# Weight and mixed-row loads on ScalarE's queue, norm factors in the tile of the matrices to invert, a second buffer for masked operands, and the order by measured durations

## Chip, core and metric

The kernel runs on one core of a Trainium2 chip. The metric is the device time of one execution in microseconds (us), median of several runs. TensorE is called PE, its weight loads PEld, VectorE DVE, ScalarE ACT, GpSimd POOL and SyncE SP. PEq, ACTq or SPq before an operation means that the engine's sequencer issued it (a DMA, for example) and the engine's arithmetic stayed free. Each engine takes its instructions strictly in the order in which they stand in its own list.

## What is computed

One layer of a hybrid decoder for 1024 prompt tokens and 64 sample tokens (8 sequences of 8), all float32, with 1024 features:

```python
h = rmsnorm(x) * norm1_g
proj = h @ w_in                                   # 1024 -> 1536 (convolution) + 1792 (RWKV)
y_conv = c_b * conv3(c_c * c_x)                   # 512 columns
r, k, v, pw, pa, pg = split(lerp(p_rw, previous token, mu))
decay, a, g = small low-rank products of pw, pa, pg
for t in tokens:                                  # per head, 8 heads of 64
    S = S * decay_t - (S @ kk_t) x (kk_t * a_t) + v_t x k_t
    y_t = S @ r_t
y_rwkv = (groupnorm(y) + bonus) * g               # 512 columns
x = x + concat(y_conv, y_rwkv) @ w_out
h2 = rmsnorm(x) * norm2_g
x = x + relu(h2 @ w_ff1) ** 2 @ w_ff2             # 1024 -> 4096 -> 1024
out = rmsnorm(x) * normf_g
```

The outputs also hold the last convolution rows, the last projected row and the final states S.

## The kernel before

Each float32 product is made of three passes over rounded parts (`passes`): high times high, high times low, low times high. A weight is therefore loaded raw (`wraw`, 256 KB each), ACT writes its rounded copy `whi`, and DVE writes the rest `wlo` (`gen_load`, `gen_split`). The activations `h_hi` and `h_lo` stay in SBUF, 8 blocks of 128 features by 1088 tokens. Tokens are cut in three groups of 384, 384 and 320 (`GROUPS`). A piece of a projection is 24 matmuls into one of two PSUM banks (tag `mm`, tile `acc`), and a generator of the piece (`post_rkv`, `post_conv_c`, `post_out`, `relu2`) empties it.

The recurrence runs in chunks of 64 tokens. A unit `u` is a pair of heads `p` and a token group `g`; there are 12, in the order of `UN` (unit 0 is p 0, g 0; unit 11 is p 3, g 2), and units 2, 5, 8 and 11 also carry the 8 sample sequences. For a unit `gen_ew` makes the elementwise operands and the chunks' triangular matrices `LT`. Those go to DRAM (`lt_d`) and come back as `M`, one small matrix a partition (`SP.dma_start(M[24 * i:24 * i + nb], lt_d[:nb])`, L920). POOL inverts them in 31 pairs of instructions (`wtmp`, `W`, L1016 and L1018, `gen_invert`); SP stores the result (`w_d`, L1023) and brings it back as `Tt` (L1042, `gen_merge`). There is one tile `M`. `gen_recur` then walks through the chunks: PE writes `rc`, DVE takes `X` from it, PE goes on, ACT scales `UT` (L1100) and prepares `GD` (L1092), PE adds, and DVE writes the new state `Gh`. One chunk's result is the next one's operand. After the chunks PE writes `py`, and `gen_finish` normalizes it (its product `gt` goes to the DRAM matrix `mix_d`; `pty` is its transpose on PE). `gen_sample` handles the 8 sequences: for each half of them it masks two operands (`VM`, L1203) and multiplies each (`pgs`, L1210). The tile `VM` has one buffer, which the prompt's last state `So` and the operand `XY` also use.

After the last units, `gen_rows` loads the rows of `mix_d` that ACT and DVE split into `h_hi` and `h_lo` again (`mr`, L1299, 18 loads of 160 or 192 KB; `gen_mixed`, `split_row`). The output projection (PE, L659) adds to `x1`, whose old values `gen_norm2` loads (`x`, L1341). `gen_norm2` then frees the pools of the recurrence, opens new ones, and loads the norm factors `gB` (512 KB, L82), which `gen_xn` multiplies in (`xn`, L374). `gen_h` transposes `xn` on PE (`pt`, L394), and the MLP follows. From about 790 us on, the MLP's loops are written plainly and have no planner.

The order of all instructions up to there comes from a planner, `Weave`: every generator yields `ck(engine, cost)` before it issues an instruction, and the planner takes whichever step can start first by those costs, its credits of buffers (`acq`) and marks (`deps`). The costs are numbers written in the source. All DMAs named above stand on SP's queue. `wv.dma(kb)` charges SP 0.5 for one.

Of the kernel before, what the change touches and what calls it, by code (L numbers as in the profile page):

```python
# [9 lines left out]
F32 = mybir.dt.float32  # L10
# [6 lines left out]
D = 1024  # L17
# [16 lines left out]
def tile_kernel(ctx: ExitStack, tc: tile.TileContext, io: dict):  # L34
# [204 lines left out]
    def lerp(acc, m, g, out, acq=()):  # L239

        s, n = GROUPS[g]
        npr = n if g < 2 else 256
        mu = vec("mu", m)
        yield ck("ACT", 0.45, acq=acq, deps=["vec", "mss"] if g == 2 else ["vec"])
        out = out()
        A.activation(out[:, :n], acc[:, :n], AF.Copy, scale=omu[:, m:m + 1])
        yield ck("DVE", 0.65 + 0.075 * g)
# [288 lines left out]
    def split_row(k, g, src):  # L536

        s, n = GROUPS[g]
        yield ck("ACT", 0.42)
        A.copy(h_hi[:, k, s:s + n], src)  # L540
        yield ck("DVE", 0.5, nb=True)
        V.tensor_tensor(h_lo[:, k, s:s + n], src, h_hi[:, k, s:s + n].bitcast(F32), op=ALU.subtract)
        wv.mark(("hr", g, k))

    def post_conv_c(j, g):
        def f(acc):
            s, n = GROUPS[g]
            yield ck("ACT", 0.38)
            if g == 0:
                cs["cc"] = pa.tile([128, NT], F32, tag="cc", name="cc")  # L550
                cs["up"] = pa.tile([128, SEQ + 2], F32, tag="up", name="up")
                cs["us"] = pa.tile([128, NB, TB + 2], F32, tag="us", name="us")
                V.memset(cs["up"][:, 0:2], 0.0)
                V.tensor_copy(cs["us"][:, :, 0:2], scT[:, :, :, j])
            A.copy(cs["cc"][:, s:s + n], acc[:, :n])
        return f

    def post_conv_x(j, g):
        def f(acc):
# [4 lines left out]
            yield ck("DVE", 0.5)  # L564
# [9 lines left out]
            for x in (1, 2):  # L574
                yield ck("DVE", 0.5)
# [7 lines left out]
    def post_conv_b(j, g):  # L583
        def f(acc):
            s, n = GROUPS[g]
            cc = cs["cc"]
            yield ck("DVE", 0.5)
# [46 lines left out]
    def gen_split(loads):  # L634

        for ld in loads:
            for i, (pl, t, src) in enumerate(ld.parts):
                yield ck("ACT", 0.55, acq=("w" + t,), deps=[("raw", id(ld), i)] + START.pop(0))
                hi, lo = (pl["pq"].tile(list(src.shape), F32R, tag=n + t, name=n, bufs=WB[t]) for n in ("whi", "wlo"))
                A.copy(hi, ld.raw[i])  # L640
                yield ck("DVE", 0.6, nb=True)
# [3 lines left out]
                wv.free("wra" + t, after=1.0)  # L645
# [85 lines left out]
    def gen_open():  # L731

        yield ck("NO", 0, deps=[(nm, p, g) for nm in ("w2", "a2", "g2") for p in range(4) for g in range(3)] + ["masks"])
        plx.close()
        at["pp"] = pp = pool("pp", ppx)
# [6 lines left out]
        at["M"] = pp.tile([96, 32, 32], F32, name="M")  # L742
# [69 lines left out]
    def gen_ew(u):  # L812
# [7 lines left out]
        yield ck("DVE", 0.5, deps=[("sgta", u)])  # L820
# [18 lines left out]
        yield ck("DVE", 0.99, deps=[("xk", p, g)] + ([("pb", u - 2)] if u > 1 else []))  # L839
# [5 lines left out]
        yield ck("DVE", 0.5, deps=[("ptk", u - 1)] if u else [])  # L845
# [3 lines left out]
        yield ck("DVE", 0.5)  # L849
        q = Em  # L850
        V.scalar_tensor_tensor(q[:, :n], xk[:, :n], vec("kk", p), Em[:, :n], op0=ALU.mult, op1=ALU.mult)
        yield ck("DVE", 0.5)
# [5 lines left out]
        yield ck("DVE", 1.0, deps=done(u - 3) + ([("B", u - 2)] if u > 1 else []))  # L858
# [7 lines left out]
        yield ck("DVE", 0.6, deps=[("xr", p, g)])  # L866
# [37 lines left out]
        yield ck("SP", 0.9)  # L904
# [12 lines left out]
        yield ck("SP", 1.8, nb=True, deps=[("inv", u - 1)] if u else [])  # L917
# [5 lines left out]
        wv.now += 1.8  # L923
        wv.mark(("M", u))

    def gen_tokens(u):
# [31 lines left out]
        yield ck("DVE", 0.5, deps=[("A", u)])  # L958
# [4 lines left out]
        yield ck("ACT", 0.42)  # L963
        rk_hi = at["pe"].tile([128, 384], F32R, tag="kx", name="rk_hi")
        A.copy(rk_hi[:, :n], kp[:, :n])  # L965
        yield ck("DVE", 0.5)
# [8 lines left out]
        yield ck("DVE", 0.5)  # L975
# [18 lines left out]
    def gen_invert(u):  # L994
# [30 lines left out]
        wv.now += 1.8  # L1025
        wv.mark(("w_d", u))

    def gen_merge(u):
# [5 lines left out]
        yield ck("SP", 1.4, lat=5.5, deps=[("w_d", u)] + done(u - 2))  # L1034
# [103 lines left out]
    def gen_sample(u):  # L1138
# [59 lines left out]
        for b0 in range(0, NB, 4):  # L1198
            bs = slice(b0, b0 + 4)
            for x, tok in enumerate((VT, UT)):  # L1200
                yield ck("DVE", 0.35)
                VM = at["pp"].tile([128, 4, 64], F32, tag="VM", name="VM", bufs=1)
                V.tensor_tensor(VM, tok[:, c:c + 1, :].broadcast_to([128, 4, 64]),  # L1203
                                bmask[:, bs].unsqueeze(2).broadcast_to([128, 4, 64]), op=ALU.mult)
                if x == 0:
                    yield ck("PE", 0.43, acq=("rec",))
                    pg = ps.tile([128, 512], F32, tag="rec", name="pgs", bufs=2)
                else:
                    yield ck("PE", 0.43)
                PE.matmul(pg[:, 0:256], KT[:, c, x, :], VM.rearrange("p b v -> p (b v)"), start=(x == 0), stop=(x == 1))  # L1210
# [25 lines left out]
    def gen_finish(u):  # L1236
# [21 lines left out]
        yield ck("POOL", 1.3, lat=3.0)  # L1258
# [13 lines left out]
        yield ck("DVE", 0.5)  # L1272
# [3 lines left out]
        yield ck("DVE", 0.5)  # L1276
# [28 lines left out]
    def gen_rows():  # L1305

        for tag, k in ROWS:
            yield ck("SP", 0.5, acq=(tag,), deps=[("T", 10), ("mixd", 6), ("convd", 2, 0)])
# [8 lines left out]
        for g in (1, 2):  # L1317
            for _, k in ROWS:
                yield ck("SP", 0.5, acq=("mraw",), deps=[("mixd", 6 + g)])
                load_row(late["pq"].tile([128, 384], F32, tag="mr", name="mr", bufs=2), g, k)  # L1320

    def gen_mixed():

        for g in range(3):
            yield ck("NO", 0, lat=0, deps=[("acc", nmain - 3 + g)])
            for _, k in ROWS:
                yield ck("NO", 0, lat=0, deps=[("mr", g, k)])
                yield from split_row(k, g, raws.pop((g, k))[:, :GROUPS[g][1]])
                if g:
                    wv.free("mraw")  # L1330
# [155 lines left out]
    pb, p5 = late["pb"], late["p5"]  # L1486
# [110 lines left out]
    gF = pb.tile([128, D], F32, tag="gB", name="gF")  # L1597
# [61 lines left out]
```

## Time and profile before

| | us |
|---|---|
| three runs | 1537.56, 1539.78, 1541.71 |
| median | 1539.78 |
| profiled execution, its own time | 1538.91 |
| its span (first to last instruction) | 1537.0 |

| engine | busy us | share of the span |
|---|---|---|
| PE | 1461.7 | 95% |
| PEld | 1371.2 | 89% |
| DVE | 823.3 | 54% |
| ACT | 508.2 | 33% |
| POOL | 315.7 | 21% |

A share is a mean over stages with different limits. The span in 40 slices tells the stages apart: a digit is tenths of the slice, and the row PEclk is the TensorE clock that was granted, in tenths of full speed. In the trace a wait of a computing engine stands in brackets behind an instruction, with what ended it; a DMA instruction's time on SPq or ACTq is the time to issue it, not the transfer.

### The profile page before, as it was taken

The numbers are of one execution on the slowest core, as the hardware profiler recorded it, in microseconds if no ns is written. First come the engines' busy times: TensorE is split into PE (matmuls) and PEld (weight loads), VectorE is DVE, ScalarE is ACT, GpSimd is POOL, SyncE is SP. The second block draws the span as 40 slices with busy tenths as digits, with TensorE's granted clock in tenths as the row PEclk, the third lists the DMA queues.
The fourth block names the chain that finished last, engine by engine and source line by source line (L and its number), as shares of the span: only waits on it lengthen the run. The fifth ranks groups of instructions, "written<-read, shape, count | busy, mean of one in ns | idle before, by whom it ended". The sixth has DMA issues, their size and how long they took to land.

```text
span 1537.0 us, 25899 instructions
## 1 busy us (share of the span) xinstructions
PE 1461.7 (95%) x10163; PEld 1371.2 (89%) x10163; DVE 823.3 (54%) x1784; ACT 508.2 (33%) x1094; POOL 315.7 (21%) x855
## 2 busy tenths in 40 slices
PE   7999889989989999888999999999999999999997
PEld 5999779878878899788999999999999999999996
DVE  6538547856655777465644444434434344444447
ACT  6532233232323334243452223322223322233225
POOL 4023661564555446200000000000000000000004
PEclk9999859999977999898999999999999999999999
DMA  5343202321221233444321101111111111011103
GB/s 184 104 149 93 59 19 70 88 67 42 72 68 45 57 97 105 148 139 156 99 74 49 42 28 56 55 41 42 30 53 55 44 54 41 28 56 55 35 1 117
DMA packets 140292, 108.25 MB, mean 70 GB/s; under 512 B 43901, under 2 KB 131081, under 8 KB 140170
## 3 DMA queue, kind: packets, MB, share of 16 engines
q1 hardware_dynamic: 109546, 91.38, 19.9%
q10 hardware_dynamic: 30624, 15.21, 3.4%
q8 instruction: 80, 1.31, 0.4%
q14 instruction: 42, 0.34, 0.1%
HBM read 88.46 MB, written 18.09 MB: 69 GB/s over the span
## 4 chain that ended last, share of the span: by engine, by line
PE 76%; POOL 10%; DVE 4%; DMA 3%; issue 3%; SPq 2%; ACT 1%; POOLq 0%; DVEq 0%; ACTq 0%
PE acc L103 23%; PE acc L1524 16%; PE acc L652 13%; PE acc L1536 7%; PE acc L659 6%; POOL W L1018 5%; POOL wtmp L1016 5%; DMA M<-lt_d 1%; PE py L1120 1%; SPq L1023 1%; PE pw L507 1%; PE pm L885 1%; PE rc L1098 1%; PE rc L1102 1%; SPq L920 1%
## 5 line engine op out<-in xcount | busy, mean ns | idle before, releaser
L652 PE MATMUL acc<-h_hi,whi 128*128 128x384 f32 (+1 forms) x672 | 230.6, 343 | 7.1 <-DVE mp L253 6.2
L103 PE MATMUL acc<-h_lo,whi 128*128 128x320 f32 (+1 forms) x720 | 234.8, 326 | 0.0
L103 PE MATMUL acc<-h_hi,wlo 128*128 128x320 f32 (+1 forms) x720 | 234.8, 326 | 0.0
L103 PE MATMUL acc<-h_hi,whi 128*128 128x320 f32 (+1 forms) x720 | 234.7, 326 | 0.0
L652 PE MATMUL acc<-h_lo,whi 128*128 128x384 f32 (+1 forms) x672 | 229.9, 342 | 2.2 <-DVE h_lo L405 2.2
L652 PE MATMUL acc<-h_hi,wlo 128*128 128x384 f32 (+1 forms) x672 | 231.4, 344 | 0.0
L1526 DVE TENSOR_TENSOR x<-acc,x 128x512 f32<-128x512 f32 (+1 forms) x193 | 132.8, 688 | 124.9 <-PE acc L1524 124.9
L1402 DVE TENSOR_TENSOR slo<-r,shi 128x384 fp32r<-128x384 f32 (+1 forms) x96 | 51.5, 537 | 204.2 <-ACT shi L1400 204.2
L1570 POOL TENSOR_TENSOR rsf<-rsf,nhalf 128x1 f32<-128x1 f32 (+1 forms) x9 | 8.0, 888 | 741.3 <-DVE rsf L1567 740.2
L1016 POOL TENSOR_TENSOR wtmp<-W,M 96x60 f32<-96x60 f32 (+24 forms) x372 | 121.0, 325 | 168.0 <-DMA M<-lt_d 93.8
L1524 PE MATMUL acc<-f2h,shi 128*128 128x512 f32 (+1 forms) x386 | 150.2, 389 | 0.0
L1524 PE MATMUL acc<-f2h,slo 128*128 128x512 f32 (+1 forms) x386 | 150.0, 389 | 0.0
L1524 PE MATMUL acc<-f2l,shi 128*128 128x512 f32 (+1 forms) x386 | 149.9, 388 | 0.0
L652 PEld LDWEIGHTS acc<-h_hi,whi 128*128 128x128 f32 x672 | 130.1, 194 | 9.1 <-ACT rk_hi L965 7.6
L103 PEld LDWEIGHTS acc<-h_lo,whi 128*128 128x128 f32 x720 | 135.1, 188 | 0.6
L103 PEld LDWEIGHTS acc<-h_hi,whi 128*128 128x128 f32 x720 | 135.1, 188 | 0.6
L103 PEld LDWEIGHTS acc<-h_hi,wlo 128*128 128x128 f32 x720 | 135.2, 188 | 0.0
L68 ACT CAST f2h<-f2r 128x1024 fp32r<-128x1024 f32 x32 | 31.9, 1047 | 309.1 <-PE acc L1524 309.1
L652 PEld LDWEIGHTS acc<-h_lo,whi 128*128 128x128 f32 x672 | 129.8, 193 | 3.2 <-DVE h_lo L405 2.4
L652 PEld LDWEIGHTS acc<-h_hi,wlo 128*128 128x128 f32 x672 | 129.7, 193 | 1.5
L1018 POOL TENSOR_TENSOR W<-W,wtmp 96x60 f32<-96x60 f32 (+24 forms) x372 | 122.0, 328 | 29.1
L1396 ACT ACTIVATE r<-acc 128x384 f32<-128x384 f32 (+1 forms) x96 | 45.3, 472 | 150.3 <-PE acc L103 141.1
(303 smaller groups left out, 2895.6 us busy)
## 6 DMA issues: line engine op xcount, KB each, us to landing
f2r<-in_w_ff SPq DMA_DIRECT2D x32, 512.0 KB
wraw<-in_w_ff ACTq DMA_DIRECT2D x58, 256.0 KB
wraw<-in_w_in SPq DMA_DIRECT2D x52, 256.0 KB
wraw<-in_w_out SPq DMA_DIRECT2D x48, 256.0 KB
xt<-in_x_prompt SPq DMA_DIRECT2D x8, 512.0 KB
x<-in_x_prompt SPq DMA_DIRECT2D x8, 512.0 KB
out_y_prompt<-out SPq DMA_DIRECT2D x7, 512.0 KB
M<-lt_d SPq DMA_DIRECT2D x32, 96.0 KB
```

The source lines that it names most:

```text
L68: A.copy(hi, src)
L103: PE.matmul(acc[:, :n], a, b, start=(i == 0), stop=(i == 23))
L507: PE.matmul(pw[:, :n], a, b, start=(i == 0), stop=(i == m - 1))
L652: PE.matmul(acc[:, :n], a, b, start=(k == i == 0), stop=(k == 7 and i == 2))
L659: PE.matmul(acc[:n, :256], a, b, start=(k == i == 0), stop=(k == 7 and i == 2))
L1016: G.tensor_tensor(tv, W[:, 0:nr, r:r + 1].broadcast_to([96, nr, wd]), M[:, r:r + 1, r + 1:32].broadcast_to([96, nr, wd]), op=ALU.mult)
L1018: G.tensor_tensor(W[:, 0:nr, r + 1:32], W[:, 0:nr, r + 1:32], tv, op=ALU.subtract)
L1396: A.activation(r[:, :n], acc[:, :n], AF.Relu)
L1402: V.tensor_tensor(lo, r[:, :n], hi.bitcast(F32), op=ALU.subtract)
L1524: PE.matmul(acc[:, :cn], a, b, start=(j == 0), stop=(j == 3 * FB - 1))
L1526: V.tensor_tensor(x1[t][:, cols], acc[:, :cn], x1[t][:, cols], op=ALU.add)
L1536: PE.matmul(acc[:, :n], a, b, start=(j == 0), stop=(j == 3 * FB - 1))
```

## The change

`gen_load` puts the weight loads on ACT's queue, all but those of the first two projections (4 loads). The planner charges 0.05 for the issue and keeps its own clock for the transfers (`dma_a`). The 18 loads of mixed rows move to ACT in the same way. A permanent tile `gM` takes the place of `M` and of the two tiles for norm factors: the matrices to invert are its first 96 partitions, the factors of the second norm are loaded into it once the last inversion is done, and those of the final norm later. In `gen_sample` the second masked operand goes into half of `Sn` or `G0`, which hold nothing that is needed then, and both products are issued together. Around the inversion the planner no longer holds SP for 2.5 us: the mark `inv` stands at the inversion's end, and the store of `W` follows as a step of its own 2.5 us later. Some 45 costs in the planner's table are other numbers.

```diff
-        yield ck("ACT", 0.45, acq=acq, deps=["vec", "mss"] if g == 2 else ["vec"])
+        yield ck("ACT", 0.58 if g < 2 else 0.5, acq=acq, deps=["vec", "mss"] if g == 2 else ["vec"])
...
+        def dma_a(self, kb=192):
+
+            self.clk["DMA"] = max(self.clk["DMA"], self.now + 0.65) + kb / 360
+            return self.clk["DMA"] + 1.05
...
     def gen_load(loads):
 
+        for x, ld in enumerate(loads):
+            for i, (pl, t, src) in enumerate(ld.parts):
+                if x < 2:
+                    yield ck("NO", 0, acq=("wra" + t,))
+                else:
+                    yield ck("ACT", 0.05, lat=0, acq=("wra" + t,))
+                raw = pl["pq"].tile(list(src.shape), F32, tag="wraw" + t, name="wraw", bufs=2)
+                (SP if x < 2 else A).dma_start(raw, src)
...
-                wv.free("wra" + t, after=1.0)
+                wv.free("wra" + t, after=1.2)
...
+        at["gM"] = pool("pg", ctx).tile([128, D], F32, name="gM")
...
-        at["M"] = pp.tile([96, 32, 32], F32, name="M")
+        at["M"] = at["gM"][:96].rearrange("p (s t) -> p s t", t=32)
...
-        yield ck("DVE", 0.5, deps=[("sgta", u)])
+        yield ck("DVE", 0.95, deps=[("sgta", u)])
...
-        yield ck("SP", 2.5)
         wv.mark(("inv", u))
+        yield ck("NO", 0, lat=2.5)
+        yield ck("SP", 1.8)
         w_d = dp.tile([24, 32, 32], F32, tag="w_d", name="w_d", bufs=3)
...
+            VM = [at["pp"].tile([128, 4, 64], F32, tag="VM", name="VM", bufs=1), (G0 if b0 else Sn)[:, 0:4, :]]
             for x, tok in enumerate((VT, UT)):
-                yield ck("DVE", 0.35)
-                VM = at["pp"].tile([128, 4, 64], F32, tag="VM", name="VM", bufs=1)
-                V.tensor_tensor(VM, tok[:, c:c + 1, :].broadcast_to([128, 4, 64]),
+                yield ck("DVE", 0.42)
+                V.tensor_tensor(VM[x], tok[:, c:c + 1, :].broadcast_to([128, 4, 64]),
...
     def load_row(raw, g, k):
         s, n = GROUPS[g]
-        SP.dma_start(raw[:, :n], mix_d[128 * k:128 * k + 128, s:s + n])
-        wv.mark(("mr", g, k), wv.now + 2.0)
+        A.dma_start(raw[:, :n], mix_d[128 * k:128 * k + 128, s:s + n])
+        wv.mark(("mr", g, k), wv.now + 2.5)
...
             wv.mark(("x1in", t), wv.now + 2.5)
+            if t == 2:
+                yield ck("SP", 0.5, deps=[("inv", 11)])
+                bcast_row(at["gM"], io["norm2_g"][0], D)
+                late["gB"] = at["gM"]
...
-        gB = late["p5"].tile([128, D], F32, tag="f2l", name="gB", bufs=FB)
-        bcast_row(gB, io["norm2_g"][0], D)
-        late["pn2"], late["gB"] = pn2, gB
+        late["pn2"] = pn2
...
-    gF = pb.tile([128, D], F32, tag="gB", name="gF")
+    gF = at["gM"]
```

In the lists below a row is line, operation, tiles written and read, shape, and a count where equal rows follow each other. On SP's queue, around the last inversion (unit 11, whose matrices have 160 rows in `w_d`), the list before:

```order
L1341 DMA x_7659<-in_x_prompt 128x1024
L1023 DMA w_d<-W 160x1x32 x4
L1341 DMA x_7698<-in_x_prompt 128x1024
L1299 DMA mr<-mix_d 128x384
L628 DMA wraw<-in_w_out 128x2x256 x2
L1042 DMA Tt_1322<-w_d 32x5x32 x4
L628 DMA wraw<-in_w_out 128x2x256
```

The same place on SP's queue now (`gM<-in_norm_g` is the load of the second norm's factors):

```order
L1347 DMA x_7552<-in_x_prompt 128x1024
L1347 DMA x_7583<-in_x_prompt 128x1024
L82 DMA gM<-in_norm_g 128x1024
L1347 DMA x_7831<-in_x_prompt 128x1024
L1032 DMA w_d<-W 160x1x32 x4
L1347 DMA x_7870<-in_x_prompt 128x1024
L1050 DMA Tt_1314<-w_d 32x5x32 x4
```

The row and weight loads are gone from there, and the factors and one `x` load stand ahead of the store of unit 11's inverse. On ACT at the start of unit 10's chunks, the list before (`h_hi<-mr`, `-cc`, `-gt` are the split copies of rows):

```order
L1062 ACTIVATE Tt_1321<-pz 32x6x32 x2
L540 CAST h_hi<-gt 128x384
L540 CAST h_hi<-mr 128x384
L1092 ACTIVATE GD<-Gh,dc 128x64
L540 CAST h_hi<-mr 128x384
L1100 ACTIVATE UT<-rc,nneg 128x64
```

And ACT at the same place now:

```order
L1070 ACTIVATE Tt_1313<-pz 32x6x32
L636 DMA wraw<-in_w_out 128x2x256 x4
L1070 ACTIVATE Tt_1313<-pz 32x6x32
L1305 DMA mr<-mix_d 128x384 x2
L1100 ACTIVATE GD<-Gh,dc 128x64
L1108 ACTIVATE UT<-rc,nneg 128x64
L648 CAST whi<-wraw 128x512
L545 CAST h_hi<-mr 128x384
```

Four weight loads and two row loads stand among the instructions of the chunk chain. On DVE after unit 2's chunks, the list before:

```order
L1203 TENSOR_TENSOR VM<-VT,bmask 128x256
L1249 TENSOR_TENSOR yc<-py,st 128x320
L851 SCALAR_TENSOR_TENSOR Em<-xk,vecT,Em 128x384
L248 SCALAR_TENSOR_TENSOR xv<-acc,vecT,xv 128x255
...
L642 TENSOR_TENSOR wlo<-wraw,whi 128x512
L1256 TENSOR_REDUCE va<-ysq 128x5
L1257 TENSOR_SCALAR va<-va 128x5
L1203 TENSOR_TENSOR VM<-UT,bmask 128x256
```

And DVE at the same place now:

```order
L1211 TENSOR_TENSOR VM<-VT,bmask 128x256
L1255 TENSOR_TENSOR yc<-py,st 128x320
L1211 TENSOR_TENSOR Sn<-UT,bmask 128x256
L857 TENSOR_TENSOR KB<-kp,Em 128x6x64
L570 TENSOR_TENSOR up<-acc,cc 128x384
```

The second masked operand follows the first after one instruction, in a buffer of its own.

## Rows read from the trace of the kernel before

**Rows 1.** The page, 40 slices of 38.4 us: PE busy and granted clock.

```profile
PE   7999889989989999888999999999999999999997
PEclk9999859999977999898999999999999999999999
```

**Rows 2.** Windows: us; busy (xcount) PE, PEld, DVE, ACT, POOL; clock; DMA share; GB/s.

```profile
187.00:209.00 22.00, 17.58 (x78) 14.89 (x78) 9.80 (x32) 5.20 (x15) 11.46 (x41) 0.54 0.15 33
428.00:464.00 36.00, 29.40 (x219) 25.18 (x219) 19.80 (x57) 7.86 (x20) 21.74 (x72) 0.68 0.25 62
616.00:624.00 8.00, 7.90 (x87) 7.44 (x87) 3.94 (x11) 3.14 (x9) 6.44 (x21) 1.00 0.02 7
632.00:640.00 8.00, 6.37 (x84) 6.08 (x85) 2.21 (x5) 1.24 (x3) 0.00 (x0) 0.55 0.99 302
687.60:701.00 13.40, 5.38 (x28) 5.33 (x28) 4.27 (x7) 1.69 (x3) 1.11 (x2) 0.62 0.93 306
840.00:880.00 40.00, 40.00 (x225) 37.16 (x224) 18.48 (x29) 10.60 (x20) 0.00 (x0) 1.00 0.13 39
```

**Rows 3.** Waits of PE in 0 to 760 us: total us, times, longest.

```profile
PE rc L1102 <- ACT UT L1100: 13.4, 15, 7.5
PE pt L394 <- DVE rs L63: 10.3, 2, 8.0
PE pgs L1210 <- DVE VM L1203: 6.7, 4, 2.5
PE acc L652 <- DVE mp L253: 6.2, 2, 4.3
```

**Rows 4.** Timeline of DVE, POOL, SP and PE around the second norm's start.

```profile
686.94 0.58 SPq L82 DMA_DIRECT2D gB<-in_norm_g  x1
...
684.58 1.01 POOL L64 TENSOR_TENSOR rs<-rs,nhalf 128x1 f32<-128x1 f32 x1 [14.27 <-DVE rs L63]
...
694.33 1.28 DVE L374 SCALAR_TENSOR_TENSOR xn<-x,rs,gB 128x1024 f32<-128x1024 f32 x1 [8.59 <-DMA gB<-in_norm_g]
...
695.67 1.11 PE L394 MATMUL pt<-ident,xn 128*128 128x128 f32 x4 [8.02 <-DVE rs L63]
```

**Rows 5.** Timeline around masked operands: DVE of unit 11, PE of unit 5.

```profile
666.47 0.42 DVE L1203 TENSOR_TENSOR VM<-VT,bmask 128x256 f32<-128x256 f32 x1 [1.88 <-DMA out_new_wkv_p<-So]
...
399.01 0.70 PE L1210 MATMUL pgs<-VM,KT 128*128 128x256 f32 x2 [2.46 <-DVE VM L1203]
```

**Rows 6.** Filler matmuls: two of 384 columns (timeline), a run of 256 (chain).

```profile
272.72 0.34 PE L652 MATMUL acc<-h_hi,wlo 128*128 128x384 f32 x1
272.90 0.34 PE L652 MATMUL acc<-h_hi,whi 128*128 128x384 f32 x1
...
706.24 22.37 PE acc L659 x188
```

**Rows 7.** Timeline of SP, ACT and PE around the late row load.

```profile
624.40 3.60 SPq L1023 DMA_DIRECT2D w_d<-W  x4
...
628.59 0.42 SPq L1299 DMA_DIRECT2D mr<-mix_d  x1
...
632.85 0.51 ACT L540 CAST h_hi<-mr 128x384 fp32r<-128x384 f32 x1 [9.09 <-DMA mr<-mix_d]
...
633.63 0.69 PE L1102 MATMUL rc<-UT,KT 128*128 128x64 f32 x2 [7.50 <-ACT UT L1100]
```

**Rows 8.** ACT's loads in the MLP (timeline), and SP's waits for raw buffers.

```profile
802.68 0.62 ACT L68 CAST whi<-wraw 128x512 fp32r<-128x512 f32 x1 [0.31 <-PE acc L103]
804.06 0.37 ACTq L89 DMA_DIRECT2D wraw<-in_w_ff  x1
...
SPq L628 <- DVE wlo L642: 103.9, 43, 10.3
```

**Rows 9.** Timeline: SP's store of unit 0's inverse, then unit 1's matrices.

```profile
169.85 3.38 SPq L1023 DMA_DIRECT2D w_d<-W  x4
173.40 1.64 SPq L920 DMA_DIRECT2D M<-lt_d  x4
```

More of the change, by code (lines that the diff above doesn't have):

```diff
@@ L538, in split_row @@
         s, n = GROUPS[g]
-        yield ck("ACT", 0.42)
+        yield ck("ACT", 0.48)
         A.copy(h_hi[:, k, s:s + n], src)
-        yield ck("DVE", 0.5, nb=True)
+        yield ck("DVE", 0.55, nb=True)
         V.tensor_tensor(h_lo[:, k, s:s + n], src, h_hi[:, k, s:s + n].bitcast(F32), op=ALU.subtract)
@@ L547, in f @@
             s, n = GROUPS[g]
-            yield ck("ACT", 0.38)
+            yield ck("ACT", 0.52)
             if g == 0:
@@ L563, in f @@
             cv = b3(cc[:, 1024:1088])
-            yield ck("DVE", 0.5)
+            yield ck("DVE", 0.57 if g < 2 else 0.9)
             V.tensor_tensor(up[:, 2 + s:2 + s + npr], acc[:, :npr], cc[:, s:s + npr], op=ALU.mult)
@@ L586, in f @@
             cc = cs["cc"]
-            yield ck("DVE", 0.5)
+            yield ck("DVE", 0.57)
             V.tensor_tensor(cc[:, s:s + n], acc[:, :n], cc[:, s:s + n], op=ALU.mult)
@@ L838, in gen_ew @@
             A.activation(Eps[:, :, 1:9], b3(cum[:, 256:320]), AF.Exp, scale=-CDEC)
-        yield ck("DVE", 0.99, deps=[("xk", p, g)] + ([("pb", u - 2)] if u > 1 else []))
+        yield ck("DVE", 1.1, deps=[("xk", p, g)] + ([("pb", u - 2)] if u > 1 else []))
         xk = xs["k", p, g]
@@ L844, in gen_ew @@
         V.tensor_tensor(kp[:, :n], kp[:, :n], xk[:, :n], op=ALU.mult)
-        yield ck("DVE", 0.5, deps=[("ptk", u - 1)] if u else [])
+        yield ck("DVE", 0.58, deps=[("ptk", u - 1)] if u else [])
         KB = at["pe"].tile([128, 6, 128], F32, tag="KB", name="KB")
@@ L857, in gen_ew @@
             wv.defer(lambda: load_sgta(u + 1))
-        yield ck("DVE", 1.0, deps=done(u - 3) + ([("B", u - 2)] if u > 1 else []))
+        yield ck("DVE", 1.25 if g < 2 else 1.7, deps=done(u - 3) + ([("B", u - 2)] if u > 1 else []))
         AR = e["AR"] = at["ARs"][u % 3]
@@ L865, in gen_ew @@
                                        Eps[HS[h], :, 0:8], op0=ALU.mult, op1=ALU.mult)
-        yield ck("DVE", 0.6, deps=[("xr", p, g)])
+        yield ck("DVE", 0.6 if g < 2 else 0.8, deps=[("xr", p, g)])
         xr = xs["r", p, g]
@@ L922, in gen_ew @@
         wv.mark(("A", u))
-        wv.now += 1.8
-        wv.mark(("M", u))
+        wv.mark(("M", u), wv.now + 2.3)
     def gen_tokens(u):
@@ L957, in gen_tokens @@
             wv.free("tr")
-        yield ck("DVE", 0.5, deps=[("A", u)])
+        yield ck("DVE", 0.61, deps=[("A", u)])
         wv.mark(("ptk", u))
@@ L962, in gen_tokens @@
         wv.free("xr", "xk")
-        yield ck("ACT", 0.42)
+        yield ck("ACT", 0.5)
         rk_hi = at["pe"].tile([128, 384], F32R, tag="kx", name="rk_hi")
         A.copy(rk_hi[:, :n], kp[:, :n])
-        yield ck("DVE", 0.5)
+        yield ck("DVE", 0.55)
         rk_lo = at["pe"].tile([128, 384], F32R, tag="rkl", name="rk_lo")
@@ L974, in gen_tokens @@
         wv.mark(("pb", u))
-        yield ck("DVE", 0.5)
+        yield ck("DVE", 0.56)
         xs.pop(("v", p, g))
@@ L1024, in gen_invert @@
         e["w_d"] = w_d
-        wv.now += 1.8
-        wv.mark(("w_d", u))
+        wv.mark(("w_d", u), wv.now + 2.0)
     def gen_merge(u):
@@ L1033, in gen_merge @@
         nb = 4 * nch
-        yield ck("SP", 1.4, lat=5.5, deps=[("w_d", u)] + done(u - 2))
+        yield ck("SP", 1.8, lat=4.5, deps=[("w_d", u)] + done(u - 2))
         LT, w_d = e["LT"], e["w_d"]
@@ L1199, in gen_sample @@
             bs = slice(b0, b0 + 4)
+            VM = [at["pp"].tile([128, 4, 64], F32, tag="VM", name="VM", bufs=1), (G0 if b0 else Sn)[:, 0:4, :]]
             for x, tok in enumerate((VT, UT)):
-                yield ck("DVE", 0.35)
-                VM = at["pp"].tile([128, 4, 64], F32, tag="VM", name="VM", bufs=1)
-                V.tensor_tensor(VM, tok[:, c:c + 1, :].broadcast_to([128, 4, 64]),
+                yield ck("DVE", 0.42)
+                V.tensor_tensor(VM[x], tok[:, c:c + 1, :].broadcast_to([128, 4, 64]),
                                 bmask[:, bs].unsqueeze(2).broadcast_to([128, 4, 64]), op=ALU.mult)
[L1205 to L1210, printed above, removed]
+            yield ck("PE", 0.87, acq=("rec",))
+            pg = ps.tile([128, 512], F32, tag="rec", name="pgs", bufs=2)
+            for x in range(2):
+                PE.matmul(pg[:, 0:256], KT[:, c, x, :], VM[x].rearrange("p b v -> p (b v)"), start=(x == 0), stop=(x == 1))
             yield ck("DVE", 0.7)
@@ L1275, in gen_finish @@
         wv.free("rec")
-        yield ck("DVE", 0.5)
+        yield ck("DVE", 0.56)
         gt = gts.pop(u)
@@ L1329, in gen_mixed @@
                 if g:
-                    wv.free("mraw")
+                    wv.free("mraw", after=0.6)
             wv.mark(("rows", g))
@@ L1345, in f @@
             n = TOK[t][1]
-            yield ck("DVE", 0.35, deps=[("x1in", t)])
+            yield ck("DVE", 0.43, deps=[("x1in", t)])
             x = x1[t][:n, 256 * q:256 * q + 256]
@@ L1484, in tile_kernel @@
                 fill(pieces)])
-    pb, p5 = late["pb"], late["p5"]
+    p5 = late["p5"]
     late["stack"].close()
```

34 lines of the change are left out of this document (15 added, 19 removed).

## The prediction, made before the change was run

> **What bounds the kernel now.** I read the page's slices first [rows 1]. From about the 21st slice on PE is at 9 in every digit and the clock is full: the MLP, where a window shows PE busy for 40.00 of 40.00 us [rows 2]. The change touches nothing that PE waits for there, so that half stays as it is. In the first half PE has digits of 7 and 8, and where it has them the clock often falls too: 187 to 209 us runs at 0.54 and 428 to 464 us at 0.68 of full speed [rows 2]. That is the lower of PE's two levels (1.2 GHz instead of 2.4) for most of the stretch, and the engine had been waiting ahead of each such stretch. So a wait of PE costs itself and then part of what PE does next at the lower level.
>
> Then I asked who ends PE's waits [rows 3]. Three are long enough to be worth an edit: one of 7.5 us on ACT's `UT`, one of 8.0 us ahead of the second norm's transposes, and four ahead of `pgs`, 6.7 us together. The rest is spread: the other waits on `UT` (13.4 less 7.5, so 5.9 us) and those on `mp` (6.2 us). Beside them stand two stretches with no filler matmuls of a projection at all [rows 2], in which PE goes through the chunk chain alone.
>
> **A, norm factors loaded early.** PE waits 8.02 us at 695.67, that is from 687.65 on. The row names `rs`, but POOL has `rs` ready at 684.58 + 1.01 = 685.6, and DVE's `xn` starts only at 694.33, released by the load of `gB`, which SP issued at 686.94 behind the close of the old pools [rows 4]. With the factors in `gM` before that, `xn` ends near 685.6 + 1.28 = 686.9, ahead of PE. So the wait goes, and with it the low clock behind it: 5.38 us busy at 0.62 between 687.6 and 701 [rows 2] is 5.38 x 0.38 = 2.0 us lost. Whole price 10.0 us. I take **-9**, since the transposes now stand elsewhere in PE's list. Ends: -10 and -4, since what `xn` waits for behind `gB` (its own tile in the new pools) is hidden by it, and half is as far as I let that go.
>
> **B, the second masked operand.** The four waits are one at the start of each sample unit; the longest is 2.46 us [rows 5], the others 4.3 us together, so some 1.4 each [rows 3]. They don't come from the operands' sharing a buffer with each other, but from sharing it with `So`: DVE waits 1.88 us until the store of `So` has left it [rows 5]. That stays, for the first operand keeps this buffer. What helps is the list: between the last `py` of units 2, 5, 8 and 11 and the first `pgs` stand 22, 9, 19 and 39 fillers, and stood 11, 6, 10 and 13. At 0.174 us each for 384 columns, and 22.37 / 188 = 0.119 for 256 [rows 6], that covers 1.9, 0.5, 1.6 and 3.1 us more. The second operand comes some 0.7 us after the first, and both products now stand together. Left over: 0.2, 2.7, 0.5 and 0; gain **-3.3**. Ends: 0 and -6.7.
>
> **C, row loads on ACT.** The 7.5 us came so: SP stood at the store of `W` (`w_d`) until POOL was done, so the row load behind it was issued at 628.59, ACT's copy of that row could start at 632.85, and `UT` stood behind the copy on ACT [rows 7]. PE then ran at 0.55 from 632 to 640: 6.37 x 0.45 = 2.9 us more [rows 2]. The whole is 10.4 us. On ACT the row loads no longer stand behind the store. But at unit 10's start four weight loads (1.05 MB) now stand ahead of two row loads on that queue; at 302 GB/s with the DMA engines 0.99 busy [rows 2] they take 3.5 us, where the row before stood behind one load of 0.52 MB (1.7 us). From issue to copy I expect 632.85 - 628.59 = 4.3, plus 1.8, so 6.1 us, of which GD, UT and one weight copy on ACT cover about 2. That leaves 4 us of wait once, and some 2.4 at the ten later loads: **-4**. Ends: -10.4, and +4 if all six pairs wait 2.4 us.
> At this place the Trainium skill speaks against the change: DMA: Bandwidth & Descriptors, section Issuing engines are not separate DMA queues, says that transfers started from several engines share the same 16 DMA engines, and that only the time to start them is saved. By that rule alone C would be 0 and the sum 1528. The trace agrees on the sharing (0.99 busy when loads pile up) but not on what the wait was made of: from 616 to 624 the DMA engines were busy 0.02 [rows 2] while SP stood still, so it was a place in a list and not bandwidth.
>
> **D, what SP's list puts later.** The store of unit 11's inverse now stands behind the factors and one `x` load, 1.05 MB or 3.5 us at the same rate. Between unit 10's `py` and unit 11's first `pz` stand 87 fillers (10.4 us at 0.119) where there were 17; the planner put them there without knowing of the 3.5. I take **+2**, ends 0 and +3.5. For units 1 and 5 the matrices now go ahead of the store of the unit before: the store loses 1.64 us of issue, the matrices gain 3.38 [rows 9]. Both are on the path in 187 to 209, so 0, ends -3.4 and +1.6.
>
> **E, issuing on ACT.** 120 loads move (48 of `w_in`, 48 of `w_out`, 6 of `w_ff1`, 18 rows) at 0.37 us of ACT's sequencer each [rows 8], where the planner has 0.05. ACT is busy a third of the time, so most are beside other work: where ACT then has nothing late, they cost nothing. 33 of them stand between two `UT` of one chain. All on the path would be 33 x 0.37 = 12.2 us, none would be 0; a chunk takes 22 / 6 = 3.7 us [rows 2] in which ACT's part is short, so one in five: 2.5, and 0.5 for the four issues between the two halves of `Tt`. **+3**, ends 0 and +12.
>
> **F, the table of costs.** Counted in the lists, the stretches of PE without any filler hold 42, 8 and 39 matmuls of the chain before, and 42, 15, 24 and 9 now. From 428 to 464 PE lost 6.6 idle and 29.4 x 0.32 = 9.4 to the clock [rows 2], 16.0 for 39, so 0.41 each: -15, +7 and +9 of them come to +0.4 us. The big holes are only moved. What better costs can win is the spread waits, 5.9 + 6.2 us; I take a third, **-4**. The `mp` wait around 175 us stays, since DVE's and ACT's lists there read alike. Ends -15 and +10, about one hole of 16 us less or two thirds of one more, since every place in the first half is dealt anew.
>
> **Sum** against the profiled execution's own 1538.9 us (0.9 below the median): -9 - 3.3 - 4 + 2 + 3 - 4 = -15.3, so 1523.6, say **1524**.
>
> **Rivals.** (1) ACT takes over SP's waits; slower. SP waited 103.9 us in 43 waits for `wlo`, before it could load into that buffer [rows 8]. SP had nothing else to do; ACT has `UT` behind it. The nearest row of this on ACT is the MLP: the copy ends at 803.30 and the load is issued at 804.06, a wait of 0.76. Add 0.37 and multiply by 33: 37.3 us in place of E's 3, so **1558**. It decides from 18.3 / 33 = 0.55 us per load on. Against it: the planner now lets 1.2 us pass between `wlo` and the load, and PE's fillers are slower than its costs, so that DVE has room. 0.12.
> (2) The late row stays late on ACT: C is +4, D +3.5, F 0, so 1538.9 - 9 - 3.3 + 4 + 3.5 + 3 = **1537**, no change. For it: six loads issued in a bunch, with 3 MB of `x` and factors beside them. 0.16.
> (3) The factors weren't the last thing that `xn` waited for, and `So` keeps the masks late: A -4, B 0, F 0: **1536**. 0.05.
> (4) The new order wins a hole as well: C -10.4 and F -15: **1506**. For it: by the end of unit 11 PE has done 101 more fillers than before, which have to be done anyway. Against it: as many chain matmuls without fillers as before. 0.20.
>
> **How the numbers follow.** The forecast (1512 to 1532) has 0.47. About 0.3% (4.6 us) is what a measurement of this kernel can tell from no change. Faster by more than that: 0.47 + 0.20 and a little of (2) and (3), 0.70; within it 0.18; slower 0.12. All ends on the good side give 1493, all on the bad side 1566; the range leaves out both corners and the far half of rival 1: 1500 to 1546.
>
> **What would show it.** A: no wait above 1 us ahead of the first `pt` of the second norm, and full clock behind it. B: waits of `pgs` on masks under 4 us in all, the longest in unit 5. C: ACT's waits for `mr`, and whether one of PE's waits on `UT` is over 3 us. D: a wait of `pz` of unit 11. E: waits of ACT's load issues for `wlo` inside the chain, well under 0.55 us each. F: the windows without fillers at a low clock again, three or four of them. Were the MLP's windows to differ, or a long PE wait to stand behind an ACT load of weights, the prediction would be wrong in its base or by rival 1.

## The result, and the profile after

The changed kernel takes 1551.76 us (1550.63 to 1554.55) against 1539.37 us of the kernel before: ratio 1.0082, 95% interval 1.0062 to 1.0102, so slower by about 12.6 us. The forecast was 1524 us, the range ended at 1546.

The page after, 40 slices of 38.7 us, PE busy and granted clock (compare [rows 1]):

```profile
PE   7999889989978899799999999999999999999997
PEclk9999859989978989599999999999999999999999
```

New is the 17th slice (620 to 658 us), with a 7 of PE and a clock of 5 tenths. In windows (columns as in [rows 2]): two stretches without fillers as before, the MLP, and two stretches that come up below. The second list is the trace of before, in the window of the last one:

```profile
187.00:212.00 25.00, 20.80 (x144) 17.98 (x145) 9.48 (x32) 4.55 (x13) 13.41 (x51) 0.53 0.16 37
431.00:475.00 44.00, 30.01 (x202) 26.54 (x203) 26.49 (x80) 12.58 (x36) 22.32 (x69) 0.65 0.25 61
...
840.00:880.00 40.00, 40.00 (x234) 38.41 (x233) 16.45 (x28) 13.13 (x24) 0.00 (x0) 1.00 0.17 53
533.00:551.00 18.00, 9.91 (x40) 8.35 (x39) 7.22 (x19) 0.46 (x1) 4.43 (x15) 0.72 0.15 36
618.00:652.00 34.00, 22.95 (x166) 21.21 (x165) 8.36 (x22) 6.84 (x18) 18.29 (x60) 0.51 0.61 191
```

```profile
618.00:652.00 34.00, 26.40 (x292) 25.12 (x292) 15.15 (x39) 9.88 (x24) 6.45 (x18) 0.85 0.51 157
```

The MLP is as it was. But from 618 to 652 us PE did, by busy time times clock, 22.95 x 0.51 = 11.7 us of full-speed work, where before it did 26.40 x 0.85 = 22.4 (an estimate). Waits of PE from 0 to 760 us (compare [rows 3]) and, last row, from 690 us on:

```profile
PE rc L1110 <- ACT UT L1108: 14.4, 14, 5.6
PE pgs L1216 <- DVE VM L1211: 9.7, 3, 7.7
...
PE acc L660 <- DVE mp L253: 4.3, 1, 4.3
...
PE pt L399 <- DVE rs L63: 0.3, 1, 0.3
```

The wait ahead of the second norm's transposes is gone (8.0 before, 0.3 now), but the masks' longest wait grew from 2.5 to 7.7 us, and one long wait on `UT` (7.5 us) became two (3.7 and 5.6 us).

**The masks of unit 8.** POOL, SP, DVE and PE after, with start and duration:

```profile
536.97 0.21 POOL L1026 TENSOR_TENSOR W<-W,wtmp 96x8 f32<-96x8 f32 x1
...
537.21 3.27 SPq L1032 DMA_DIRECT2D w_d<-W  x4
540.58 1.19 SPq L1139 DMA_DIRECT2D out_new_wkv_p<-So  x2
...
532.24 0.28 DVE L1136 COPY So<-ptg 64x128 f32<-64x128 f32 x1 [0.71 <-PE py L1204]
...
543.12 0.42 DVE L1211 TENSOR_TENSOR VM<-VT,bmask 128x256 f32<-128x256 f32 x1 [9.98 <-DMA out_new_wkv_p<-So]
...
543.60 1.22 PE L1216 MATMUL pgs<-VM,KT 128*128 128x256 f32 x2 [7.66 <-DVE VM L1211]
```

`So` was ready at 532.5. Its store stands on SP behind the store `w_d` of unit 9's inverse, and that one waits until POOL's inversion ends at 537.2. The mask `VM` wants the buffer of `So`, so DVE, and with it everything behind the mask on DVE, stood for 9.98 us. Over the four sample units DVE's waits for that store, first after, then before:

```profile
DVE VM L1211 <- DMA out_new_wkv_p<-So: 17.1, 4, 10.0
```

```profile
DVE VM L1203 <- DMA out_new_wkv_p<-So: 7.8, 4, 2.6
```

**The scaled copies of unit 10.** ACT, SP, POOL and PE after:

```profile
619.72 1.95 ACTq L636 DMA_DIRECT2D wraw<-in_w_out  x4
...
621.80 3.88 ACTq L1305 DMA_DIRECT2D mr<-mix_d  x2
625.72 0.35 ACT L1100 ACTIVATE GD<-Gh,dc 128x64 f32<-128x64 f32 x1 [3.68 <-DMA wraw<-in_w_out]
...
640.43 0.20 POOL L1024 TENSOR_TENSOR wtmp<-W,gM 96x8 f32<-96x8 f32 x1
...
640.65 0.33 SPq L82 DMA_DIRECT2D gM<-in_norm_g  x1
...
644.76 0.39 ACTq L636 DMA_DIRECT2D wraw<-in_w_out  x1
645.20 0.31 ACT L1108 ACTIVATE UT<-rc,nneg 128x64 f32<-128x64 f32 x1 [10.93 <-DMA gM<-in_norm_g]
...
645.56 0.69 PE L1110 MATMUL rc<-UT,KT 128*128 128x64 f32 x2 [5.62 <-ACT UT L1108]
```

`UT` doesn't read the norm factors. What stood was the weight load in front of it, for 10.9 us, and the compiled lists with each instruction's semaphores (counters on which an instruction waits, and which count up when a transfer has landed) say why. ACT, and SP's load of the factors:

```
569 L1100 ACTIVATE GD<-Gh,dc 128x64 [waits DVE_49]
570 L545 CAST h_hi<-mr 128x384 [waits DMAHW2_49]
571 L636 DMA wraw<-in_w_out 128x2x256 [waits DMAHW7_49,DVE_49]
572 L1108 ACTIVATE UT<-rc,nneg 128x64 [waits PE_49]

329 L82 DMA gM<-in_norm_g 128x1024 [waits DMAHW3_49,DMAHW7_49,DMAHW1_49,Pool_49]
```

The program has eight completion semaphores for transfers, DMAHW0 to DMAHW7, dealt in turn to the transfers of both queues in the order in which the planner emitted them. A transfer waits until the one that had its semaphore last has landed. The factors count on DMAHW7, and the weight load of row 571 is the eighth transfer after them. So ACT waited for a transfer that SP starts only when POOL has read `gM` for the last time. Of the 120 loads on ACT, 71 carry such a wait for a transfer of SP. The 3.68 us in front of `GD` are a turn as well, within ACT's own queue: the second of the two row loads at 621.80 is the eighth transfer after one of the weight loads at 619.72.

### The profile page after: what moved, and what is told of

Its sections match the earlier page's. It is cut to its first block, busy times and chain, and to the rows that moved or that the text cites. A ratio compares the mean times of both kernels' runs of the same rounds, so it can differ in the third digit from the quotient of the medians.

```text
span 1548.9 us, 25877 instructions
## 1 busy us (share of the span) xinstructions
PE 1464.8 (95%) x10163; PEld 1372.5 (89%) x10163; DVE 823.4 (53%) x1784; ACT 508.6 (33%) x1094; POOL 313.2 (20%) x855
## 4 chain that ended last, share of the span: by engine, by line
PE 81%; POOL 8%; DVE 3%; DMA 2%; issue 2%; ACT 2%; SPq 1%; POOLq 0%; ACTq 0%; DVEq 0%
PE acc L103 23%; PE acc L660 18%; PE acc L1531 16%; PE acc L1543 7%; PE acc L667 6%; POOL W L1026 4%; POOL wtmp L1024 3%; PE py L1128 1%; PE pm L894 1%; DMA gM<-lt_d 1%; PE pw L512 1%; PE rc L1110 1%; PE rc L1095 1%; PE rc L1106 1%; PE rc L1098 1%
## 5 line engine op out<-in xcount | busy, mean ns | idle before, releaser
L1024 POOL TENSOR_TENSOR wtmp<-W,gM 96x60 f32<-96x60 f32 (+24 forms) x372 | 119.3, 321 | 192.3 <-DMA gM<-lt_d 111.6
```

The source lines that it names most:

```text
L1024: G.tensor_tensor(tv, W[:, 0:nr, r:r + 1].broadcast_to([96, nr, wd]), M[:, r:r + 1, r + 1:32].broadcast_to([96, nr, wd]), op=ALU.mult)
```

## Experiments

Each ratio is against the kernel before, run beside it (medians 1539.8 to 1540.7 us); differences in us are the ratio's, of 1540.

### From the changed kernel backwards

Theory Q: ACT stands at its load issues and holds back `UT`. Theory S: the masks wait for the store of `So`, which stands behind `w_d`. Theory N: the new order itself loses.

**Rows back on SP's queue.**

```diff
-        A.dma_start(raw[:, :n], mix_d[128 * k:128 * k + 128, s:s + n])
+        SP.dma_start(raw[:, :n], mix_d[128 * k:128 * k + 128, s:s + n])
```

> The changed kernel with the mixed rows of L1305 back on SP's queue and nothing else moved; the weight loads stay on ScalarE's queue. Theory Q (ScalarE's in-order queue stands at its load issues and holds back the scaled copies UT behind them): of the two UT waits of unit 10 in the changed kernel (3.68 us at 622.8, 5.62 us at 640.0) the first has two row loads ahead of it and goes, the second has a weight load ahead of it and stays; 3.7 us and a part of the half-clock stretch are saved, 1545 to 1549 us. Theory N (the new order of the instructions loses the time itself, the queue is not its cause): both waits stay, 1549 to 1554 us.

1540.72 us, ratio 1.0000 (0.9988 to 1.0011): 12.6 us less than the change, outside what either theory had expected, and both `UT` waits are gone (longest 0.6 us), also the one that was to stay. With the rows elsewhere the turns of the semaphores fall otherwise: the weight load in front of the same `UT` now has DMAHW3, which another load of ACT had.

**All loads back on SP's queue**, in the order that was planned for ACT.

```diff
-                (SP if x < 2 else A).dma_start(raw, src)
+                SP.dma_start(raw, src)
```

(and the edit above)

> The changed kernel with the mixed rows and all weight loads back on SP's queue; PE, VectorE, GpSimd and ScalarE's other work keep their order. Theory Q: both UT waits of unit 10 (9.3 us together) go, and with them most of the 34 us at half clock that follow (some 10 us of loss beyond what the kernel before has there); 1531 to 1538 us. Against it stands SP, which waits for GpSimd's inversions with the loads behind it, as before: up to 5 us back. Theory N: 1548 to 1554 us, with PE late at the same places for other reasons.

1538.69 us, ratio 0.9985 (0.9974 to 0.9997): 14.9 us less than the change, 0.7 us above Q's range and far from N's. The waits on `UT` fall from 14.4 to 6.6 us, and the masks' wait stays, as S has it:

```profile
PE pgs L1216 <- DVE VM L1211: 7.9, 2, 6.3
PE rc L1110 <- ACT UT L1108: 6.6, 14, 1.1
```

**`So` in a buffer of its own.**

```diff
-            PE.transpose(pt[0:64, 0:128], st, ident)
+            for hs in HS: PE.matmul(pt[hs, 0:64], st[hs], ident[hs, hs], start=True, stop=True)
...
-            So = at["pp"].tile([64, 128], F32, tag="VM", name="So")
-            V.tensor_copy(So, pt[0:64, 0:128])
+            So = at["pp"].tile([128, 64], F32, tag="So", name="So")
+            V.tensor_copy(So, pt[:, 0:64])
```

> The changed kernel with the carried state's output tile So in a buffer of its own instead of the mask's buffer VM (the two heads are transposed to the two halves of a 128x64 tile, so that it fits). Theory S (the mask VM of unit 8 waits for the store of So, which SP starts only after the w_d stores of unit 9, which wait for GpSimd): the 7.66 us wait at 536 us goes, and the 10.2 us at half clock behind it cost up to 5 us less; 1538 to 1545 us. Rival: unit 9 can't go on before its inversion is done at about 541 us, so PE waits there for something else; 1548 to 1553 us.

1542.62 us, ratio 1.0014 (1.0001 to 1.0027): 10.5 us less than the change. No wait on `VM` is left, and in the window of unit 8 PE is busy 16.56 us at full clock, where it was 9.91 us at 0.72:

```profile
533.00:551.00 18.00, 16.56 (x141) 14.70 (x142) 13.05 (x37) 3.06 (x6) 5.02 (x12) 1.00 0.31 77
```

S holds.

**Both.**

> Both of the last two edits: loads back on SP's queue, So in a buffer of its own. If theories Q and S both hold and their gains add up: 1518 to 1530 us, faster than the kernel before. If the new order itself loses (theory N): 1540 us or more.

1528.87 us, ratio 0.9930 (0.9911 to 0.9948). The two gains nearly add up (14.9 and 10.5; 23.4 together), and N falls: the order that was planned for the change is 10.8 us faster than the kernel before once ACT is rid of the loads and the masks of `So`.

**The turns of the semaphores shifted**, with all loads left on ACT.

```diff
-            load_x(late["px"], t)
+            load_x(late["px"], t, 1 + 4 * (t == 3))
...
-        SP.dma_start(x1[t][:n], tok_rows(io["x_prompt"], io["x_sample"], t))
+        for i in range(parts): SP.dma_start(x1[t][i * n // parts:(i + 1) * n // parts], tok_rows(io["x_prompt"], io["x_sample"], t)[i * n // parts:(i + 1) * n // parts])
```

> The changed kernel with one load of a residual tile (the x of L1347 that SP issues right behind the norm factors) split into five parts of 25 or 26 partitions; ScalarE's queue keeps all its loads. Eight completion semaphores are dealt in turn to the transfers of both queues, and a transfer waits for the last one that had its semaphore. In the changed kernel the weight load ahead of UT at 645 us is the eighth transfer after the norm factors, which SP issues only when the last inversion is done; with four more transfers between, the turns fall otherwise. Theory Q in this form: the 5.6 us wait for UT goes, the 3.7 us wait at 623 us (a row load behind a weight load of its own queue) stays, and a part of the half-clock stretch goes: 1540 to 1546 us. Rival: it is the 512 KB of the norm factors and the loads themselves that crowd the DMA engines, whichever semaphore they have: 1549 to 1554 us.

1548.31 us, ratio 1.0048 (1.0032 to 1.0065): 5 us less, not the 6 to 12 expected, and the interval touches that of the change (from 1.0062). So the place of the wait tells more than the time: the wait of 5.6 us at 645 us is gone, but some 7.5 us later stands another. SP, ACT and PE of this kernel:

```profile
642.16 6.46 SPq L1347 DMA_DIRECT2D x<-in_x_prompt  x5
...
651.85 0.33 ACTq L1305 DMA_DIRECT2D mr<-mix_d  x1
652.21 0.62 ACT L648 CAST whi<-wraw 128x512 fp32r<-128x512 f32 x1 [5.72 <-DMA x<-in_x_prompt]
...
653.10 0.69 PE L1110 MATMUL rc<-UT,KT 128*128 128x64 f32 x2 [4.97 <-ACT UT L1108]
```

In this program the row load of 651.85 is the eighth transfer after the last of the five parts of `x`, and it starts when that part has landed. The miss thus bears the theory out: which ACT load stands, and for which transfer, follows the turns and not the data. The rival (the factors crowd the DMA engines) would have left the wait at 645 us where it was. The time itself lies between the two ranges and decides nothing.

### The parts of the change, alone

**The loads on ACT's queue alone**, weights and rows, with the planner's entries for them.

```diff
-                SP.dma_start(raw, src)
+                (SP if x < 2 else A).dma_start(raw, src)
```

> The kernel before with one part of the change alone: weight loads and mixed rows on ScalarE's queue, with the planner's entries for them. Theory Q: ScalarE now stands at loads whose semaphore a transfer of SP has that waits for GpSimd, and PE waits for UT, VT or weights behind it; 1543 to 1560 us. The prediction's terms C and E: rows 4 us earlier, 3 us of issue time, so 1535 to 1540 us.

1549.76 us, ratio 1.0064 (1.0047 to 1.0082): 9.9 us slower. ACT's longest wait and PE's behind it, in unit 10 again:

```profile
643.59 0.35 ACT L1100 ACTIVATE GD<-Gh,dc 128x64 f32<-128x64 f32 x1 [10.58 <-DMA Tt<-w_d]
...
644.52 0.69 PE L1110 MATMUL rc<-UT,KT 128*128 128x64 f32 x2 [6.75 <-ACT UT L1108]
```

`GD` doesn't read `Tt` either; four loads of ACT stand in front of it, with turns behind transfers of `w_d`, `x` and `Tt`.

**The early norm factors alone.**

```diff
+            if t == 2:
+                yield ck("SP", 0.5, deps=[("inv", 11)])
+                bcast_row(at["gM"], io["norm2_g"][0], D)
```

(and `gM` in the place of `M`)

> The kernel before with the norm factors in the tile of the matrices to invert alone, loaded ahead of the last unit's w_d on SP. The prediction's terms A and D: the wait of the second norm's first transpose goes (9 us), SP's factor load and one x load ahead of w_d cost up to 3.5 us; 1530 to 1534 us. Rival: the next thing is late there and takes the gain over; 1537 to 1541 us.

1528.46 us, ratio 0.9927 (0.9911 to 0.9943): 11.2 us faster, more than expected. From 670 to 760 us PE has no wait above 0.2 us.

**The new durations alone.**

```diff
-        yield ck("DVE", 0.5, deps=[("sgta", u)])
+        yield ck("DVE", 0.95, deps=[("sgta", u)])
```

(and the other costs, with the new steps around the inversion)

> The kernel before with the new durations in the planner alone; loads on SP's queue, one masked operand, factors late. The order on SP puts the store of So behind the w_d of unit 9 here too. Theory S: the masks of unit 8 wait for it, 7 us and some loss of clock, and what the table gains elsewhere (the prediction's 4 us) does not make up for it; 1541 to 1549 us. Rival, the table gains by itself: 1532 to 1538 us.

1547.30 us, ratio 1.0040 (1.0025 to 1.0054): 6.2 us slower. The longest of the masks' waits is the one of S, in unit 8; the waits on `UT`, of which the longest was 7.5 us before, are short:

```profile
PE pgs L1209 <- DVE VM L1202: 12.5, 4, 8.5
...
PE rc L1101 <- ACT UT L1099: 5.0, 13, 0.4
```

In this kernel the row loads are still on SP, but the new order puts most of those around unit 10 ahead of the last `w_d`. So the late row that the prediction's term C was to cure is gone without a move to ACT.

**The second masked operand alone.**

```diff
+            VM = [at["pp"].tile([128, 4, 64], F32, tag="VM", name="VM", bufs=1), (G0 if b0 else Sn)[:, 0:4, :]]
```

(and both products issued together, as in the change)

> The kernel before with the second buffer for the masked operands alone. The prediction's term B: of 6.7 us of waits on the masks 3.3 us go; 1534 to 1538 us. Rival (what hides the wait is short there, or the planner's order shifts elsewhere): 1538 to 1542 us.

1560.46 us, ratio 1.0125 (1.0112 to 1.0139): 19.3 us slower, the dearest part, and neither the expectation nor its rival had it. SP, DVE and PE in unit 5, and a later wait of PE:

```profile
406.31 3.27 SPq L1023 DMA_DIRECT2D w_d<-W  x4
409.69 1.17 SPq L1131 DMA_DIRECT2D out_new_wkv_p<-So  x2
...
412.17 0.43 DVE L1203 TENSOR_TENSOR VM<-VT,bmask 128x256 f32<-128x256 f32 x1 [13.18 <-DMA out_new_wkv_p<-So]
...
412.65 1.22 PE L1208 MATMUL pgs<-VM,KT 128*128 128x256 f32 x2 [12.15 <-DVE VM L1203]
...
480.54 0.90 PE L1269 MATMUL pty<-ident,yn 128*128 128x128 f32 x3 [10.91 <-DVE yn L1263]
```

It is S again, twice: the steps of the masks cost other numbers, the planner deals everything behind them anew, and the store of `So` comes to stand behind `w_d` in units 5 and 8. In the list of the kernel before it stood ahead of the next `w_d`. The wait at 480 us is another: DVE's `yn` needs a small power on POOL (`va`), which stands in POOL's list behind a whole inversion.

**The new durations with `So` apart.** Edit: the two above, of the durations and of `So`.

> The kernel before with the new durations in the planner, and So in a buffer of its own; nothing else of the change. Theory S: what the table lost by itself was the store of So behind w_d, so the 8.5 us wait of unit 8 goes with the half-clock stretch behind it; 1535 to 1541 us, no slower than the kernel before. Rival, the table's order loses elsewhere too: 1543 to 1548 us.

1534.47 us, ratio 0.9955 (0.9941 to 0.9968): 13.1 us less than without the buffer. The durations gain 6.9 us once S is out of the way.

### Parts together

**Factors and second mask.**

> The kernel before with the early norm factors and the second masked operand, without the new durations and without the queue. The sum of the two terms as measured apart (factors 11.4 us, mask 0 to 3 us): 1525 to 1529 us.

1552.55 us, ratio 1.0072 (1.0060 to 1.0085). Missed, as the mask alone was: PE's two waits of S, in units 5 and 8, are here too, the longest 12.6 us.

**The same with `So` apart.**

> The last kernel with So in a buffer of its own. In the order of the kernel before the store of So stands ahead of the w_d of the next inversion, so theory S expects little: what the masks of units 5 and 8 still wait (1.5 to 3 us); 1522 to 1528 us.

1536.87 us, ratio 0.9968 (0.9955 to 0.9980): 16.0 us less than without the buffer, but missed. The masks no longer wait, yet the kernel is still 6.3 us slower than with the factors alone: with the old durations other waits take the place, and the second mask gains nothing.

```profile
PE pty L1270 <- DVE yn L1264: 21.8, 3, 12.2
PE rc L1103 <- ACT UT L1101: 13.5, 9, 10.3
...
DVE yn L1264 <- POOL va L1258: 19.6, 4, 8.0
```

DVE waits 19.6 us for `va` on POOL, again behind an inversion. The 10.3 us on `UT` are the late row of [rows 7]: ACT stood 10.94 us for an `mr` that SP loads behind the last `w_d`.

**Factors, durations and `So` apart.**

> The kernel before with the early norm factors, the new durations and So in a buffer of its own: no second masked operand, no loads on ScalarE's queue. If the measured parts add up (factors 11.4 us; durations with So 6.2 us): 1521 to 1525 us. Rival: both gain at the same place, the second norm, and don't add: 1527 to 1531 us.

1529.64 us, ratio 0.9921 (0.9905 to 0.9937). The gains of 11.2 and 6.9 us don't add up: 12.2 together, as the rival had it.

**The same with the second mask**: all of the change but the loads on ACT's queue, and `So` apart.

> The last kernel with the second masked operand, so all of the change but the loads on ScalarE's queue, planned for SP, and So in a buffer of its own. The prediction's term B, once the store of So is out of the masks' way: 3 us less than the last kernel, 1518 to 1522 us. Rival: with So apart the masks no longer bound anything and the order shifts by chance: within 3 us of the last kernel or later, as the 1528.9 us of the changed kernel with its loads moved back suggest.

1521.77 us, ratio 0.9886 (0.9866 to 0.9906): 17.6 us faster than the kernel before, the fastest of all. PE in the window of above, now with hardly a wait and at full clock; unit 10 starts earlier in this kernel, and its low clock stands ahead of that window:

```profile
602.00:616.00 14.00, 13.63 (x125) 12.52 (x126) 5.68 (x13) 4.65 (x12) 11.48 (x33) 0.51 0.75 258
...
618.00:652.00 34.00, 33.36 (x366) 32.49 (x365) 20.99 (x53) 13.31 (x32) 9.93 (x23) 1.00 0.57 174
```

So the way from the kernel before to the changed one goes in four steps of runs: everything but the queue, with `So` apart -17.6 us; planning the order for loads on ACT +6.8; the loads on ACT +12.9; `So` in the masks' buffer +10.5; together +12.6. Why the order planned for ACT costs 6.8 us even with the loads on SP wasn't separated. The trace of the kernel with both edits shows one place, in unit 8, where the second mask stands on DVE behind a `yn` that waits for `va`; in the fastest kernel PE has no wait for a mask:

```profile
537.05 0.72 DVE L1271 TENSOR_TENSOR yn<-yc,va 64x192 f32<-64x192 f32 x2 [5.35 <-POOL va L1265]
...
538.26 1.22 PE L1216 MATMUL pgs<-Sn,KT 128*128 128x256 f32 x2 [3.68 <-DVE Sn L1211]
```

## Why the prediction was wrong

**What bounds the kernel** held: the MLP's window is the same, and what was lost was lost ahead of it, in waits of PE and at the low clock. Without C and E the terms of the sum come to -14.3 us, and that part measured -17.6 once `So` stood apart. What failed is the rest: `So` in the masks' buffer (+10.5), which the sum had at nothing, and C and E with the order planned for them (+12.9 + 6.8), which the sum had at -1.

**A** was right in its mechanism: the wait for `rs` is 0.3 us where it was 8.0 [rows 4], and no low clock follows. Alone, with D in it, it brought 11.2 us, where the prediction had -9 + 2 = -7. **D** cost PE nothing where it was looked for: PE has no wait on `pz` after 640 us. But the factors' load that D put there is the transfer for which ACT then stood.

**B** failed, at the sentence "That stays, for the first operand keeps this buffer." The wait for `So`'s store [rows 5] was taken as a fixed 1.9 us, and only the fillers that cover it were counted. But it is the place of that store on SP that sets it, and the prediction compared SP's list around the inversions without asking where this store had gone. It had gone behind a `w_d` that waits for POOL: +10.5 us in the changed kernel, 13.1 with the durations alone, 16.0 with factors and mask. With `So` apart the second mask brings 5.4 us in the new order (ratios 0.9921 and 0.9886, whose intervals touch), not far from the 3.3; with the old durations it costs 6.3 us even so (0.9927 and 0.9968). Rival 3 had `So` keep the masks late too, but as dear as before (B 0).

**C and E** failed in E. The row loads did come off SP: ACT's longest wait for `mr` is 2.5 us where it was 9.1 [rows 7]. But the new durations alone had already cut the longest wait on `UT` from 7.5 to 0.4 us, so that C had nothing left to win beside F. And E priced a load on ACT by the 0.37 us of its issue [rows 8] and found 0 to 12 us; what it costs is the wait in front of the issue, which in ACT's list holds back `GD` and `UT`. The queue cost 9.9 us alone and 12.9 in the new order, so C and E together are about +10 to +13 and not -1. The Trainium skill states this reading: Perfetto Trace Analysis, section DMA Instruction — HWDGE (DVE, Sync), says that the profiler's start of a DMA instruction is the moment when its semaphores are satisfied, so that a wait is not in its duration. The trace agrees: the load at 644.76 shows 0.39 us, and the 10.93 us stand in the brackets of the next instruction. The prediction also weighed the Trainium skill's rule in DMA: Bandwidth & Descriptors, section Issuing engines are not separate DMA queues, by which C would be 0. The runs measure C and E only together, and show a loss.

**Rival 1** had ACT stand at its loads with `UT` behind, and the outcome lies between the forecast's and its 1558 us. The prediction's own sign for it came true, a long wait of PE behind a weight load on ACT. But it had the cause in `wlo`, 0.76 us at each of 33 loads. In the trace few loads stand long, and the longest (10.9 us, unit 10) is released by a transfer of SP. The chance of 0.12 was weighed against the wrong wait.

**F** had the sign right only with `So` apart: then the durations gain 6.9 us (forecast 4). With `So` in the masks' buffer they lose 6.2 us, since their order too puts its store behind `w_d`. The stretches without fillers came again as foreseen (0.53 and 0.65 of the clock), and the `mp` wait around 175 us stayed (4.3 us).

So two of the sum's terms failed for the same reason: a step on SP's queue that waits for POOL (`w_d`, the factors) was costed for itself, and not for what stands behind it, once by its place in the list and once by a shared semaphore.

## What to carry to other kernels

A store or load has a place in its queue, and whoever reuses its buffer waits for all that stands ahead of it: when an order is dealt anew, look up each transfer whose buffer is shared, and what the transfer in front of it waits for. On an engine that computes, a DMA issue is a possible wait for everything behind it: list the semaphores of each issue, not its 0.4 us. Measure parts of a change apart, and also with the suspected wait taken out: here the durations lost 6 us alone and gained 7 once 256 bytes a partition had been spent on `So`. The second mask lost 19 us alone, still lost 6 beside the factors with `So` apart, and gained 5 only in the order by the new durations.

## What was not expected of the hardware

The granted clock was 0.51 over the whole of 618 to 652 us, so half speed (1.2 GHz) nearly throughout. The two waits of 3.7 and 5.6 us didn't bring it down: it had fallen by 620 us, ahead of the first, after PE had been busy for 4.81 of 8 us. And it stayed at half from 628 to 640 us, between the two, with PE busy for 11.95 of 12 us:

```profile
612.00:620.00 8.00, 4.81 (x71) 4.12 (x71) 7.00 (x16) 2.14 (x5) 2.63 (x9) 0.91 0.51 107
620.00:628.00 8.00, 3.37 (x15) 2.99 (x15) 1.04 (x3) 1.52 (x5) 6.36 (x22) 0.50 0.96 331
628.00:640.00 12.00, 11.95 (x97) 10.66 (x96) 5.07 (x12) 3.27 (x8) 9.73 (x30) 0.50 0.34 110
```

The fastest kernel has such a stretch too, 14 us from 602 on at 0.51 with PE busy for 13.63 of them, but not 34. As an estimate the low clock took 22.95 x 0.49 = 11.2 us of PE's work between 618 and 652 us, more than the two waits (9.3 us). How much of that the waits caused isn't shown.
